# Rotary embedding on one core: first batch stored in three parts instead of five, and one signed GpSimd product per tile instead of two

## Chip, cores and metric

One core of one Trainium2 chip. The metric is the device time of one execution in microseconds (us); lower is better. The times are medians of several executions. Profiles come from one execution each; their span starts at the first instruction and is about 1.9 us shorter than the device time.

## The reference, cut to what matters

```python
x: (8, 2048, 8, 64) float32      # batch, sequence, heads, head width
cos, sin: (2048, 32) float32
x1, x2 = x[..., :32], x[..., 32:]
out1 = x1 * cos - x2 * sin
out2 = x1 * sin + x2 * cos
out  = concatenate([out1, out2], axis=-1)
```

The input is 33.55 MB, the output as much, and the two tables 0.52 MB. Each element needs two products and an add, so the work is thin beside the bytes.

## The kernel before

A batch is a tile of 128 partitions; a partition holds 16 sequence positions, a row of 32 KB (`ROW`). `HD` is one position (2 KB), `UNIT` four positions (8 KB a row). Batches live in five buffers (`NBUF`); a batch is rotated in place and stored from its buffer, so the load of batch b + 5 waits until batch b is stored. SyncE issues the loads, ScalarE the stores.

```python
cos_sb = const_pool.tile([P, R, Dh], f32, tag="cb")
sin_sb = const_pool.tile([P, R, Dh], f32, tag="sb")
nsin   = const_pool.tile([P, R, Dh], f32, tag="ns")
...
keep(nc.scalar.mul(nsin, sin_sb, -1.0))
...
def rotate(b, lo, n):            # one tile of 2 or 4 positions
    ...
    if kind != "C":              # GpSimd: t2 = swapped halves of x, times -sin and sin
        for u, tab in ((1, sin_sb), (0, nsin)):
            keep(nc.gpsimd.tensor_mul(
                out=t2u[:, :, u, :]..., in0=xu[:, :, 1 - u, :]..., in1=rep(tab[...], H)))
    keep(nc.vector.tensor_mul(out=t1..., in0=xk, in1=rep(cos_ps[...], 2 * H)))
    if kind == "A":
        keep(nc.vector.tensor_add(out=xt, in0=t1, in1=t2))
    ...                          # B: add on TensorE; C: both products on VectorE, add on TensorE

for b in range(B):
    done = 0
    outs = list(spans([2 * UNIT, UNIT, UNIT] if b == last else [ROW]))
    for lo, n in spans(pieces(b)):       # first batch: 2, 2, 4, 4, 4 positions
        rotate(b, lo, n)
        done = lo + n
        while outs and sum(outs[0]) <= done:
            whole = outs.pop(0)
            if b == 0:
                for part in spans([HD, HD, 2 * HD, UNIT, 2 * UNIT]):
                    store(b, *part)
            else:
                store(b, *whole)
    if b + NBUF <= last:
        load(b + NBUF)
```

Each tile's form is fixed per batch: most are "A"; five tiles are "B" or "C". `t1` of form A and the cosine table used by VectorE are in PSUM.

## Time and profile before

| | before |
|---|---|
| median | 163.64 us (3 runs, 163.50 to 163.69) |
| span of the profile | 161.9 us |
| VectorE busy | 140.1 us |
| GpSimd busy | 139.0 us |
| bytes moved | 67.65 MB, mean 418 GB/s |
| last add ends / last store lands | 152.5 / 161.0 us |

Three resources are busy nearly all the time. Which one sets the end is read from what is still at work last, and from what is queued when it starts: the prediction shows the strip of slices, the queues, the stretches and the waits for that. In these views PE is TensorE (PEld its weight loads), DVE VectorE, ACT ScalarE, POOL GpSimd and SP SyncE; a q behind the name is the engine's queue of instructions that only issue or wait. A line of a stretch has the stretch and its length, busy time and number of instructions of PE, PEld, DVE, ACT and POOL, the granted TensorE clock, the DMA share and GB/s.

### The profile page before, as it was taken

What the parts mean: (1) busy time and instruction counts of PE and PEld (TensorE: products, weight loads), DVE (VectorE), ACT (ScalarE), POOL (GpSimd) and SP (SyncE); (2) the same over time, 40 slices, a digit from 0 to 9 for tenths busy, and PEclk for the clock granted to TensorE, in tenths of its full rate; (3) what the DMA queues carried; (4) which work ended last, traced back from release to release, by engine and by line L of the source; (5) the groups of instructions that cost most, each with busy time, mean ns of one, the idle gap of its engine ahead of it and who ended that gap; (6) DMA issues with size and microseconds to landing.
All of it is one profiled execution on the core that took longest, in us unless ns stands there. A gap on an engine that the chain in (4) does not pass through costs nothing.

```text
span 161.9 us, 470 instructions
## 1 busy us (share of the span) xinstructions
PE 46.7 (29%) x80; PEld 18.6 (11%) x80; DVE 140.1 (87%) x66; ACT 14.4 (9%) x24; POOL 139.0 (86%) x70
## 2 busy tenths in 40 slices
PE   0000000498009950893039903970000000000000
PEld 0000000142004310340023402320000000000000
DVE  0468999999999999999999999999999999999600
ACT  3300000014000220041001210130000000000000
POOL 1299999999999899999994999999999999996000
PEclk9999999999955796599755985899555555555555
DMA  5999999999998989998999999989999999999994
GB/s 188 417 435 505 438 413 413 413 421 437 437 470 344 465 364 445 494 413 389 510 397 389 518 391 397 502 389 407 494 397 413 486 397 421 478 397 409 429 417 178
DMA packets 3746, 67.65 MB, mean 418 GB/s; under 512 B 416, under 2 KB 416, under 8 KB 1056
## 3 DMA queue, kind: packets, MB, share of 16 engines
q1 hardware_dynamic: 1728, 34.08, 49.6%
q10 hardware_dynamic: 2016, 33.56, 48.3%
q14 instruction: 2, 0.02, 0.0%
HBM read 34.08 MB, written 33.55 MB: 418 GB/s over the span
## 4 chain that ended last, share of the span: by engine, by line
DVE 75%; POOL 9%; issue 6%; DMA 3%; SPq 0%; DVEq 0%; POOLq 0%
DVE t L128 40%; DVE xt L135 33%; POOL t L121 9%; DMA sin_sb<-in_sin_dram 3%; DVE t L145 3%; DVEq L135 0%; SPq L69 0%; SPq L67 0%; POOLq L121 0%
## 5 line engine op out<-in xcount | busy, mean ns | idle before, releaser
L121 POOL TENSOR_TENSOR t<-xt,sin_sb 128x1024 f32<-128x1024 f32 (+1 forms) x32 | 71.1, 2222 | 8.6 <-DMA sin_sb<-in_sin_dram 5.6
L128 DVE TENSOR_TENSOR t<-xt,cos_ps 128x2048 f32<-128x2048 f32 (+1 forms) x34 | 73.4, 2167 | 0.8
L121 POOL TENSOR_TENSOR t<-xt,nsin 128x1024 f32<-128x1024 f32 (+1 forms) x32 | 71.2, 2225 | 0.0
L135 DVE TENSOR_TENSOR xt<-t,t 128x2048 f32<-128x2048 f32 (+1 forms) x29 | 62.2, 2145 | 5.4 <-POOL t L121 2.5
L140 PE MATMUL o<-t,eye 128*128 128x512 f32 x24 | 17.1, 804 | 25.0 <-DVE t L128 25.0
L156 PE MATMUL o<-t,eye 128*128 128x512 f32 x16 | 10.9, 786 | 36.6 <-DVE t L128 36.6
L141 PE MATMUL o<-t,eye 128*128 128x512 f32 x24 | 15.2, 719 | 0.0
L142 ACT COPY xt<-o 128x512 f32<-128x512 f32 x12 | 7.0, 586 | 46.5 <-PE o L141 46.5
L140 PEld LDWEIGHTS o<-t,eye 128*128 128x128 f32 x24 | 5.6, 250 | 33.4 <-issue 33.4
L161 ACT COPY xt<-o 128x512 f32<-128x512 f32 x8 | 4.7, 586 | 42.7 <-DVE t L128 26.6
L156 PEld LDWEIGHTS o<-t,eye 128*128 128x128 f32 x16 | 3.6, 248 | 41.5 <-POOL t L121 30.4
L141 PEld LDWEIGHTS o<-t,eye 128*128 128x128 f32 x24 | 6.0, 251 | 8.5 <-issue 8.5
L92 DVE COPY cos_ps<-cos_sb 128x512 f32<-128x512 f32 x1 | 0.7, 695 | 6.1 <-DMA cos_sb<-in_cos_dram 6.1
L157 PE MATMUL o<-t,neye 128*128 128x512 f32 x8 | 4.9, 722 | 0.2 <-DVE t L145 0.2
L145 DVE TENSOR_TENSOR t<-xt,sin_ps 128x2048 f32<-128x2048 f32 x2 | 4.6, 2280 | 0.0
L157 PE MATMUL o<-t,eye 128*128 128x512 f32 x8 | 4.1, 592 | 0.0
L157 PEld LDWEIGHTS o<-t,neye 128*128 128x128 f32 x8 | 1.8, 239 | 3.7 <-issue 3.7
L157 PEld LDWEIGHTS o<-t,eye 128*128 128x128 f32 x8 | 1.5, 190 | 1.9 <-issue 1.9
L89 ACT ACT_TABLE_LOAD x1 | 1.3, 1283 | 0.7 <-PEq L202 0.7
L89 ACT ACTIVATE nsin<-sin_sb 128x512 f32<-128x512 f32 x1 | 0.6, 630 | 4.8 <-DMA sin_sb<-in_sin_dram 4.8
L90 ACT COPY sin_ps<-sin_sb 128x512 f32<-128x512 f32 x1 | 0.6, 579 | 0.0
L79 POOL MEMSET eye<- 128x128 f32 x1 | 0.2, 205 | 0.3 <-POOLq L202 0.3
(6 smaller groups left out, 1.0 us busy)
## 6 DMA issues: line engine op xcount, KB each, us to landing
xt<-in_x_dram SPq DMA_DIRECT2D x7, 4096.0 KB, 26.7
out_dram<-xt ACTq DMA_DIRECT2D x6, 4096.0 KB, 33.3
out_dram<-xt ACTq DMA_DIRECT2D x2, 2048.0 KB, 24.3
out_dram<-xt ACTq DMA_DIRECT2D x3, 1024.0 KB, 11.2
xt<-in_x_dram SPq DMA_DIRECT2D x2, 1024.0 KB, 5.9
xt<-in_x_dram SPq DMA_DIRECT2D x1, 2048.0 KB, 11.4
out_dram<-xt ACTq DMA_DIRECT2D x2, 256.0 KB, 18.9
out_dram<-xt ACTq DMA_DIRECT2D x1, 512.0 KB, 32.6
```

What stands on the lines that cost most here:

```text
L89: keep(nc.scalar.mul(nsin, sin_sb, -1.0))
L92: keep(nc.vector.tensor_copy(cos_ps, cos_sb))
L121: nc.gpsimd.tensor_mul(out=t2u[:, :, u, :].rearrange("p (r h) d -> p r h d", h=H), in0=xu[:, :, 1 - u, :].rearrange("p (r h) d -> p r h d" ...
L128: nc.vector.tensor_mul(out=t1.rearrange("p (r k d) -> p r k d", r=nr, d=Dh), in0=xk, in1=rep(cos_ps[:, r0 : r0 + nr, :], 2 * H),)
L135: keep(nc.vector.tensor_add(out=xt, in0=t1, in1=t2))
L140: nc.tensor.matmul(o, eye, t1[:, cs], start=True, stop=False)
L141: nc.tensor.matmul(o, eye, t2[:, cs], start=False, stop=True)
L142: keep(nc.scalar.copy(xt[:, cs], o))
L145: nc.vector.tensor_mul(out=t2.rearrange("p (r k d) -> p r k d", r=nr, d=Dh), in0=xk, in1=rep(sin_ps[:, r0 : r0 + nr, :], 2 * H),)
L156: nc.tensor.matmul(o, eye, t1u[:, gs, u, :], start=True, stop=False)
L157: nc.tensor.matmul(o, eye if u else neye, t2u[:, gs, 1 - u, :], start=False, stop=True)
L161: nc.scalar.copy(xu[:, gs, u, :], o.rearrange("p (g d) -> p g d", d=Dh))
```

## The change

The intent: get the first batch out earlier and in fewer pieces, so that its buffer takes the sixth batch's load earlier; and halve GpSimd's instruction count by multiplying both swapped halves in one go with a table that holds -sin and sin side by side. Its space is found by letting the raw tables share rotating buffers.

```diff
-    cos_sb = const_pool.tile([P, R, Dh], f32, tag="cb")
-    sin_sb = const_pool.tile([P, R, Dh], f32, tag="sb")
-    nsin = const_pool.tile([P, R, Dh], f32, tag="ns")
+    cos_sb = t1s_pool.tile([P, R, Dh], f32, tag="t1s", name="cos_sb")
+    sin_sb = t1s_pool.tile([P, R, Dh], f32, tag="t1s", name="sin_sb")
+    sgn = const_pool.tile([P, R, 2, Dh], f32, tag="sg")
...
-    keep(nc.scalar.mul(nsin, sin_sb, -1.0))
+    for lo, hi in ((0, 4), (4, R)):
+        keep(nc.scalar.mul(sgn[:, lo:hi, 0, :], sin_sb[:, lo:hi, :], -1.0))
+        keep(nc.scalar.copy(sgn[:, lo:hi, 1, :], sin_sb[:, lo:hi, :]))
...
-            for u, tab in ((1, sin_sb), (0, nsin)):
-                keep(nc.gpsimd.tensor_mul(... one half ...))
+            keep(
+                nc.gpsimd.tensor_mul(
+                    out=t2.rearrange("p (r h u d) -> p r h u d", r=nr, h=H, u=2),
+                    in0=swapped(xt, nr),        # steps by -Dh between the halves
+                    in1=signed(sgn[:, r0 : r0 + nr, :, :], nr),
+                )
             )
...
+    def shares(b):
+        if b == 0:
+            return [HD, 7 * HD, 2 * UNIT]
...
-        outs = list(spans([2 * UNIT, UNIT, UNIT] if b == last else [ROW]))
+        outs = list(spans(shares(b)))
...
-                whole = outs.pop(0)
-                if b == 0:
-                    for part in spans([HD, HD, 2 * HD, UNIT, 2 * UNIT]):
-                        store(b, *part)
-                else:
-                    store(b, *whole)
+                store(b, *outs.pop(0))
```

More of the change, by code (lines that the diff above doesn't have):

```diff
@@ L95, in rep, with swapped, signed @@
         return dataclasses.replace(a, ap=[a.ap[0][:], a.ap[1][:], [0, n], a.ap[-1][:]])
+    def swapped(a, nr):
+        return dataclasses.replace(
+            a,
+            offset=a.offset + Dh,
+            ap=[a.ap[0][:], [HD, nr], [D, H], [-Dh, 2], [1, Dh]],
+        )
+    def signed(a, nr):
+        return dataclasses.replace(
+            a, ap=[a.ap[0][:], [D, nr], [0, H], [Dh, 2], [1, Dh]]
+        )
     kinds = {}
@@ L118, in rotate @@
         if kind != "C":
-            for u, tab in ((1, sin_sb), (0, nsin)):
-                keep(
-                    nc.gpsimd.tensor_mul(
-                        out=t2u[:, :, u, :].rearrange("p (r h) d -> p r h d", h=H),
-                        in0=xu[:, :, 1 - u, :].rearrange("p (r h) d -> p r h d", h=H),
-                        in1=rep(tab[:, r0 : r0 + nr, :], H),
-                    )
+            keep(
[3 more added lines that the diff above has]
+                    in1=signed(sgn[:, r0 : r0 + nr, :, :], nr),
                 )
+            )
         keep(
@@ L171, in pieces @@
         return [UNIT] * 4
+    def shares(b):
+        if b == 0:
+            return [HD, 7 * HD, 2 * UNIT]
+        if b == last:
+            return [2 * UNIT, UNIT, UNIT]
+        return [ROW]
     for b in range(B):
         done = 0
-        outs = list(spans([2 * UNIT, UNIT, UNIT] if b == last else [ROW]))
+        outs = list(spans(shares(b)))
         for lo, n in spans(pieces(b)):
```

## The prediction

> **What bounds the kernel now.** I read the strip of 40 slices first, then the DMA queues, then stretches of time, and only then the chain of waits, because the three busy rows compete for the title.
>
> ```profile
> DVE  0468999999999999999999999999999999999600
> POOL 1299999999999899999994999999999999996000
> DMA  5999999999998989998999999989999999999994
> DMA packets 3746, 67.65 MB, mean 418 GB/s; under 512 B 416, under 2 KB 416, under 8 KB 1056
> q1 hardware_dynamic: 1728, 34.08, 49.6%
> q10 hardware_dynamic: 2016, 33.56, 48.3%
> ```
>
> VectorE, GpSimd and the DMA engines all look full. But DVE and POOL end two to three slices (of 4.05 us) before the DMA row does, and the two DMA queues (q1 loads, q10 stores) together take 97.9% of 16 engines' span. Only 2.1% of 161.9 us, 3.4 us, is not covered by packets. The stretches say where that is (columns at the end: DMA share, GB/s):
>
> ```profile
> 2.00:14.00 12.00, 0.00 (x0) 0.00 (x0) 6.35 (x6) 1.37 (x4) 7.11 (x5) 1.00 1.03 429
> 44.00:58.00 14.00, 9.08 (x14) 3.85 (x15) 13.65 (x7) 1.76 (x3) 13.53 (x6) 0.63 0.96 398
> 66.00:124.00 58.00, 26.49 (x48) 10.61 (x46) 56.22 (x26) 7.04 (x12) 55.59 (x25) 0.74 1.01 434
> 124.00:152.00 28.00, 0.00 (x0) 0.00 (x0) 26.97 (x14) 0.00 (x0) 24.23 (x13) 0.50 1.00 430
> 159.00:162.00 3.00, 0.00 (x0) 0.00 (x0) 0.00 (x0) 0.00 (x0) 0.00 (x0) 0.50 0.19 79
> ```
>
> A packet is counted in the stretch in which it starts, so edges blur a little. The transfers run at about 430 GB/s from 2 us to 159 us, whether loads and stores mix (66 to 124) or only stores are left (124 to 152). 67.65 MB at the 434 of the long stretch are 155.9 us. The first packet starts at 1.7 us and the last ends at 160.6 us (packet records), 158.9 us: about 3 us above the ideal. By the packet records one part of those is 0.5 us of slow first rows at the head, another 0.55 us of stretched load rows, nearly all of it between 40 and 58 us (the 398 above), the rest row overhead and uneven ends of the 16 engines.
>
> The chain of waits says something else:
>
> ```profile
> DVE 75%; POOL 9%; issue 6%; DMA 3%; SPq 0%; DVEq 0%; POOLq 0%
> DVE t L128 40%; DVE xt L135 33%; POOL t L121 9%; DMA sin_sb<-in_sin_dram 3%; DVE t L145 3%; DVEq L135 0%; SPq L69 0%; SPq L67 0%; POOLq L121 0%
> ```
>
> It is a chain of compute and ends with the last add, at 152.5 us; that store's own time is the rest of the span. A 1 MB store needs 2.4 us at 434 GB/s, yet the last one lands 8.5 us after its issue (the shortest issue-to-landing time of any store), because earlier stores are queued before it. The DMA queue sets the end. Compute has about 3 to 5 us of slack: the last store has only to be in the queue when the one before it drains, at about 157 us.
>
> The first batch's stores, by issue and landing (KB each, us to landing), and SyncE's waits:
>
> ```profile
> 10.66 17.84 ACTq L74 DMA_DIRECT2D out_dram<-xt  x5
> out_dram<-xt ACTq DMA_DIRECT2D x1, 512.0 KB, 32.6
> out_dram<-xt ACTq DMA_DIRECT2D x1, 1024.0 KB, 39.8
> out_dram<-xt ACTq DMA_DIRECT2D x1, 2048.0 KB, 35.0
> SPq L67 <- DMA out_dram<-xt: 83.2, 4, 27.9
> ```
>
> The diff's loop looks as if it issued all five parts together after the batch, but the trace has them at 10.66, 11.06, 13.25, 18.71 and 28.16 us: each goes when its rows are done. They land at 24.7, 35.0, 45.9, 58.5 and 63.2 us, and the sixth batch's load, which needs that buffer, is issued only at 63.3.
>
> **What the Trainium skill says.** "DMA: Bandwidth & Descriptors", Queues, rings and completion order: each DMA engine takes turns between the queues it has work for, packet by packet. The trace agrees: beside 32 KB load rows, the second 256 KB of stores took 10.3 us (24.7 to 35.0), 25 GB/s, about the 2:32 share of 432. The same page, Where 436 GB/s comes from, gives a ceiling of 435 GB/s; the 434 measured here leaves nothing above it. "GPSIMD Engine Reference", Performance versus the Vector engine, has 4497 ns for an fp32 product of 2048; here 1024-element products start 2.28 us apart and 512-element ones 1.215, so a line through both gives 4.41 us for 2048. "SBUF — State Buffer", Who interferes with whom: a DVE instruction with two SBUF inputs contends with GpSimd. In the code each product and add of VectorE has one input in PSUM, and both take 2292 ns beside a busy GpSimd; the change leaves that so.
>
> **The change part by part.**
>
> *Store parts.* Five row sizes (2, 2, 4, 8, 16 KB) become three (2, 14, 16). No byte is saved. Rows: 128 per DMA, eight per engine, so 16 fewer rows on each engine. A 2 KB store row takes 84 ns and a 32 KB one 1213 ns in the packet records; the line through them has 8.7 ns per row: 16 x 8.7 = 0.14 us saved. Timing: the first part goes at about 11 us as before, lands near 25. The 14 KB part is ready with the third tile, near 18.7, and is at the head of the store queue from 25 on. A turn of an engine is then one load row (1.21 us) and one 14 KB row (0.54, from the line): 1.75, eight turns 14 us, landing near 40. The 16 KB part: 8 x 1.82 = 14.6, landing near 54.5. So the first batch's store is out some 8.5 us earlier, and the sixth load is issued near 55 instead of 63.3. The store-only gap (58 to 67 us) fills with loads, and the loads end later: I count 32 load rows per engine for batches 1 to 4, 25 of them sent by 54, the rest and the later loads in turns of 2.43 us with 32 KB stores. That puts the later loads near 91, 111 and 130 us, now 86.2, 106.3 and 125.8 us. VectorE wants them near 97, 114 and 133. Still in time, with thinner margins of 3 us. Work on the path saved: 0.14 us.
>
> *The slow stretch at 40 to 58 us.* 4 and 8 KB store rows alternate there with load rows, and some load rows take up to 1.74 us instead of 1.21. From 66 to 124, where rows of 32 KB alternate, this hardly occurs. If the small rows or the drained load queue cause it, the change takes away up to 0.55 us; I don't know the cause, so I count half, 0.25 us.
>
> *One product per tile.* Two products of 1024 (4.56 us start to start) become one of 2048 (4.41 by the line): 0.15 us per four-row tile. There are 28 pairs at 1024 and 4 pairs at 512: 28 x 0.15 + 4 x 0.15 = 4.8 us of GpSimd time. All beside the DMA queue: nothing at the end.
>
> *Signed table.* GpSimd's first product starts at 6.89, when the sine lands. It will wait for two ScalarE instructions of 128 elements a row (about 0.3 us each, as the 0.30 us negation of the 128x128 identity): start near 7.4. Its first product ends near 9.7 instead of 9.37; by the fourth tile the shorter products have made it up. First store some 0.3 us later, hidden: the first store packet starts at 14.6 us now although issued at 10.66, behind load rows already under way.
>
> *Tables in rotating buffers.* The cosine and sine tables use the buffers that the second batch's VectorE-only tile takes; their readers are done near 9 us, the tile starts at 28. No wait.
>
> Sum: 163.64 - 0.14 - 0.25 = 163.25; with rounding in the uneven tail, **163.2 us**.
>
> **Rivals.**
>
> 1. *GpSimd is slower with the swapped access.* The product now reads x with a step backwards between halves, one dimension more. For: nothing in this trace has that pattern. Against: runs of 32 contiguous elements stay. Slack absorbs about 4 us, 3% of GpSimd's 139; at 10% slower the end would go out by some 10 us, to 173.
>
> 2. *Loads come late.* The margins of 3 us on the last two loads are estimates. If they vanish, VectorE idles by a few us, and the slack at the end takes most of that: 163.5 to 165.
>
> 3. *Compute is the true bound, as the chain has it.* Then the saving on GpSimd and the earlier stores would shorten the end by 1 to 3 us, to 161 or 162. Against: from 124 us stores alone fill the engines, without a gap, until the last drains.
>
> 4. *Removing the small rows frees the whole loss in mid-kernel*: 162.9.
>
> **Range and chances.** The body moves only between -0.7 us (all of the stretch and the rows) and +0.5 (thin load margins); widened below by 0.3 for something of rival 3, 162.6 to 164.1 should hold it 8 times in 10. A gain of 2% needs 3.3 us, more than every idle moment of the DMA engines together: 0.02. A loss of 2% needs rival 1 or a new wait: 0.03. Within 2%: 0.95.
>
> **What would show it.** Right: DMA still near 430 GB/s throughout and 98% in the two queues; 1728 packets on the store queue (2016, less 256 rows, less 16 semaphore packets for each of the two DMAs saved); the first batch's last part landing near 54 us; the sixth load issued near 55; no store-only stretch at 58 to 67; GpSimd busy near 134 us; VectorE's last add still near 152. Wrong: a stretch after 20 us below 400 GB/s, GpSimd products well over 4.6 us, idle VectorE before the batches of 114 and 133 us, or a last store that lands less than 5 us after its issue, which would mean that compute had become the bound.

## More of the kernel before

One more line pair is needed later: the GpSimd groups before, kept apart by shape (times executed, then busy us and mean ns of one).

```profile
L121 POOL TENSOR_TENSOR t<-xt,nsin 128x1024 f32<-128x1024 f32 x28 | 66.1, 2360 | 0.0
L121 POOL TENSOR_TENSOR t<-xt,sin_sb 128x1024 f32<-128x1024 f32 x28 | 66.0, 2356 | 3.1 <-DVE xt L135 2.6
```

Consecutive products overlap a little, so busy time over count (66 / 28) slightly overstates what one costs.

## The result and the profile after

| | before | after |
|---|---|---|
| median, same rounds | 163.66 us (6 runs, 163.50 to 163.76) | 163.67 us (6 runs, 163.52 to 164.02) |
| ratio after / before | | 1.0004, 95% interval 0.9991 to 1.0018 |
| GpSimd busy | 139.0 us | 135.8 us |
| VectorE busy | 140.1 us | 140.1 us |
| first batch's last part lands | 63.2 us | 53.8 us |
| sixth load issued | 63.3 us | 53.8 us |
| last three loads land | 86.2, 106.3, 125.8 us | 92.4, 112.4, 131.7 us |
| last add ends / last store lands | 152.5 / 161.0 us | 153.3 / 160.8 us |

A ratio here is the mean time of one kernel's fast runs over that of the other's of the same rounds, so it isn't quite the ratio of the medians beside it.

The strip and the queues after:

```profile
DVE  0458999999999999999999899999999998999900
POOL 1199999999999799989995989997999969999100
DMA  5999999899999999999999998999999999999994
...
DMA packets 3457, 67.64 MB, mean 419 GB/s; under 512 B 384, under 2 KB 384, under 8 KB 768
...
q1 hardware_dynamic: 1728, 34.08, 49.7%
q10 hardware_dynamic: 1728, 33.56, 48.3%
```

The DMA row is as full as before (98.0% in the two queues, 97.9% before), with 1728 store packets where there were 2016. GpSimd's row has more gaps (the 5 to 8) than before: it is ahead and waits. In stretches, with GB/s in the last column:

```profile
22.00:26.00 4.00, 0.00 (x0) 0.00 (x0) 3.86 (x3) 0.00 (x0) 4.00 (x2) 1.00 0.94 336
44.00:58.00 14.00, 8.97 (x16) 3.75 (x16) 13.65 (x7) 1.76 (x3) 13.12 (x3) 0.67 1.00 431
66.00:124.00 58.00, 27.13 (x48) 10.77 (x46) 55.84 (x25) 7.04 (x12) 53.58 (x13) 0.74 1.01 434
124.00:152.00 28.00, 0.00 (x0) 0.00 (x0) 26.69 (x14) 0.00 (x0) 24.51 (x7) 0.50 1.00 430
```

The same four us in the kernel before:

```profile
22.00:26.00 4.00, 0.00 (x0) 0.00 (x0) 3.86 (x3) 0.00 (x0) 4.00 (x3) 1.00 0.98 418
```

The slow stretch that was at 44 to 58 us (398 GB/s) is gone from there (431), but a new one stands at 22 to 26 us (336 instead of 418). It moved. The last long stretches are as before.

The chain of waits names other things now:

```profile
DMA 46%; DVE 36%; POOL 8%; issue 4%; SPq 1%; ACT 0%; DVEq 0%; POOLq 0%; ACTq 0%
DMA xt<-in_x_dram 24%; DVE t L141 19%; DMA out_dram<-xt 18%; DVE xt L148 16%; POOL t L134 8%; DMA sin_sb<-in_sin_dram 3%; DVE t L158 1%; SPq L69 0%; SPq L67 0%; ACT sgn L91 0%; DVEq L148 0%; ACT sgn L90 0%; POOLq L134 0%; ACTq L74 0%
```

DVE 75% became DMA 46% with the same total: the chain follows whichever wait came last by a hair, and a load was now last where before a product was. I read it as a picture of a tie, not of a new bound; the experiments below test that. Where it hangs is in the waits and in the timeline near the last load:

```profile
POOL t L134 <- DMA xt<-in_x_dram: 3.7, 4, 1.4
DVE xt L148 <- POOL t L134: 3.4, 5, 1.6
```
```profile
131.85 4.51 POOL L134 TENSOR_TENSOR t<-xt,sgn 128x2048 f32<-128x2048 f32 x1 [1.41 <-DMA xt<-in_x_dram]
153.35 0.34 ACTq L74 DMA_DIRECT2D out_dram<-xt  x1
```

GpSimd waits 1.41 us for the last batch, which lands at 131.7, some 6 us later than before; the last store is issued at 153.35 instead of 152.5, and lands at 160.8 all the same. The GpSimd groups after:

```profile
L134 POOL TENSOR_TENSOR t<-xt,sgn 128x2048 f32<-128x2048 f32 x28 | 125.9, 4525 | 7.4 <-DVE xt L148 3.8 <-DMA xt<-in_x_dram 3.7
L134 POOL TENSOR_TENSOR t<-xt,sgn 128x1024 f32<-128x1024 f32 x4 | 9.3, 2346 | 6.0 <-ACT sgn L91 6.0
```

The 28 big tiles take 125.9 us instead of 66.1 + 66.0, some 6 us less by busy time; but the two-instruction form overlapped itself, and the total of GpSimd fell by 3.2 us (139.0 to 135.8).

### The profile page after: what moved, and what is told of

Read it like the earlier page. It is cut to its first block, busy times and chain, and to the rows that moved or that the text cites. A ratio compares the mean times of both kernels' runs of the same rounds, so it can differ in the third digit from the quotient of the medians.

```text
span 161.6 us, 440 instructions
## 1 busy us (share of the span) xinstructions
PE 47.1 (29%) x80; PEld 18.7 (12%) x80; DVE 140.1 (87%) x66; ACT 15.1 (9%) x27; POOL 135.8 (84%) x38
## 3 DMA queue, kind: packets, MB, share of 16 engines
q1 hardware_dynamic: 1728, 34.08, 49.7%
q10 hardware_dynamic: 1728, 33.56, 48.3%
## 4 chain that ended last, share of the span: by engine, by line
DMA 46%; DVE 36%; POOL 8%; issue 4%; SPq 1%; ACT 0%; DVEq 0%; POOLq 0%; ACTq 0%
DMA xt<-in_x_dram 24%; DVE t L141 19%; DMA out_dram<-xt 18%; DVE xt L148 16%; POOL t L134 8%; DMA sin_sb<-in_sin_dram 3%; DVE t L158 1%; SPq L69 0%; SPq L67 0%; ACT sgn L91 0%; DVEq L148 0%; ACT sgn L90 0%; POOLq L134 0%; ACTq L74 0%
## 5 line engine op out<-in xcount | busy, mean ns | idle before, releaser
L134 POOL TENSOR_TENSOR t<-xt,sgn 128x2048 f32<-128x2048 f32 (+1 forms) x32 | 135.1, 4253 | 13.5 <-ACT sgn L91 6.0
L170 PE MATMUL o<-t,neye 128*128 128x512 f32 x8 | 5.7, 830 | 0.2 <-DVE t L158 0.2
L90 ACT ACTIVATE sgn<-sin_sb 128x128 f32<-128x128 f32 (+1 forms) x2 | 0.8, 413 | 4.8 <-DMA sin_sb<-in_sin_dram 4.8
L91 ACT COPY sgn<-sin_sb 128x128 f32<-128x128 f32 (+1 forms) x2 | 0.8, 388 | 0.0
```

The source lines that it names most:

```text
L90: keep(nc.scalar.mul(sgn[:, lo:hi, 0, :], sin_sb[:, lo:hi, :], -1.0))
L91: keep(nc.scalar.copy(sgn[:, lo:hi, 1, :], sin_sb[:, lo:hi, :]))
L134: nc.gpsimd.tensor_mul(out=t2.rearrange("p (r h u d) -> p r h u d", r=nr, h=H, u=2), in0=swapped(xt, nr), in1=signed(sgn[:, r0 : r0 + nr, ...
L170: nc.tensor.matmul(o, eye if u else neye, t2u[:, gs, 1 - u, :], start=False, stop=True)
```

## Experiments

Twelve runs on two chips, in three calls; each call has its own runs of the kernel before (11 each). Theory: the transfers set the end, so the bytes and the cost of the rows are all that counts, and compute has some us of slack. Rivals: the compute chain sets it; or the two halves of the change have opposite effects that cancel.

| run | median us | ratio to before, 95% interval |
|---|---|---|
| stores_only | 163.42 | 0.9973 (0.9938 to 1.0007) |
| product_only | 165.42 | 1.0078 (1.0033 to 1.0123) |
| product_again | 165.51 | 1.0085 (1.0037 to 1.0132) |
| after_again | 163.86 | 0.9996 (0.9969 to 1.0024) |
| copy_only | 163.04 | 0.9942 (0.9902 to 0.9983) |
| less_1mb | 161.16 | 0.9829 (0.9782 to 0.9876) |
| dve_plus1 | 163.57 | 0.9988 (0.9957 to 1.0019) |
| dve_plus4 | 169.83 | 1.0393 (1.0338 to 1.0447) |
| few_stores_before | 158.89 | 0.9693 (0.9647 to 0.9740) |
| few_stores_after | 159.37 | 0.9722 (0.9667 to 0.9776) |
| one_part | 164.64 | 1.0043 (1.0004 to 1.0082) |
| rows_2k | 183.86 | 1.1190 (1.1118 to 1.1262) |

The intervals are wider than in the first comparison because the kernel before scattered more on these chips (medians 163.83, 163.58 and 163.66; single runs up to 166.0). The medians are of all runs, the ratios of those marked fast. Four runs were marked slow, which here means only over 1.5% above the fastest of the same kernel, with a clock (0.731 to 0.745) like that of the others: one each of product_again, after_again, rows_2k and the kernel before.

### What sets the end: copy_only, less_1mb

The changed kernel without the rotation, and with 1 MB less to store:

```diff
         for lo, n in spans(pieces(b)):
-            rotate(b, lo, n)
             done = lo + n
```
```diff
+        if b == 3:
+            return [3 * UNIT]
         return [ROW]
```

> The changed kernel without any rotation: every batch is loaded and stored as it came (wrong result on purpose), same DMAs with the same rows. My theory: the transfers alone need nearly all of the time, 161 to 163.5 us. Rival B: the time falls well below, to 157 us or less, since VectorE's 146 us chain with its head and tail is gone.

> The changed kernel, but the fourth batch stores only three of its four tiles: 1 MB less to write (wrong result on purpose), all the compute kept. My theory: 1.05 MB at 433 GB/s, so 2.4 us less (161.2). Rival B: no change, since no instruction of the chain is gone.

Without any rotation: 163.04 us (162.97 to 163.14). Its page:

```profile
DVE  0100000000000000000000000000000000000000
DMA  5999999999999999999999999999999999999895
```

VectorE is idle, and the kernel is only 0.6 us faster than with 140 us of work on it. So all compute together costs some 0.6 us of the end (163.67 is of another call; the kernel before of this call is 0.8 us above). Taking away 1.05 MB took 2.5 us (163.67 to 161.16; 2.4 expected), with all compute kept, so it was not the compute chain. Their outputs are wrong, which doesn't matter for the times.

### How much slack compute has: dve_plus1, dve_plus4

One extra product on VectorE, for the first or for all four tiles of the seventh batch:

```diff
+        if b == 6 and lo == 0:           # dve_plus4: if b == 6
+            keep(nc.vector.tensor_mul(out=t1..., in0=xk, in1=rep(cos_ps[...], 2 * H)))
         if kind == "A":
```

> The changed kernel with one extra VectorE product of 2.29 us on the first tile of the seventh batch, late in the kernel (result unchanged). Transfers set the end: the last store is issued near 155.6 instead of 153.35, the store before it drains near 158, so the time stays within 0.3 us of the changed kernel. Rival (the compute chain sets the end): 2.3 us longer.

> The same extra product on all four tiles of the seventh batch, 9.2 us of VectorE (result unchanged). If transfers set the end with a slack of about 3 us in compute: the last add ends near 162.5, its store lands some 4.5 us later, so 168 to 169.5, about 5 us more. Rival (the compute chain sets the end): 9 us more, 172.5 or above.

With 2.29 us more on VectorE, late and on the chain: 163.57 us, against 163.86 of the unchanged kernel. Nothing. The last issue and its time to landing (KB, us):

```profile
155.37 0.34 ACTq L74 DMA_DIRECT2D out_dram<-xt  x1
out_dram<-xt ACTq DMA_DIRECT2D x1, 1024.0 KB, 5.3
```

The store is issued 2.0 us later and lands at 160.7, as before: it spent less time in the queue, 5.3 us instead of 7.4. That is the plainest sign of a wait that is not on the path. With 9.2 us more, 169.83 us: some 6 us came through (168 to 169.5 were expected, so the slack was a little less than I had reckoned, or the runs of 170.6 and 171.0 had another cause; only the run of 168.9 has a profile). In that one the last add ends at 162.3 and its store lands 3.9 us later. Compute sets the end there.

### What the product change is worth if compute does set the end: few_stores_before, few_stores_after

```diff
     def store(b, lo, n):
+        if 1 <= b <= 5:
+            return
```

> The kernel before without the stores of batches 1 to 5 (wrong result on purpose): 21 MB less to write, so the transfers need only some 110 us and compute must set the end. VectorE's last add near 152.3 as now, its store lands some 4 us later: 158 to 159.5 us in all. A time near 163 would mean that something else than transfers held the kernel.

> The changed kernel with the same stores left out (wrong result on purpose). VectorE's 140 us of work are the same, and GpSimd was not ahead of it by need: within 0.7 us of few_stores_before although GpSimd has 3 us less to do. If GpSimd is what paces compute (rival): 2 to 3 us faster than few_stores_before.

158.89 and 159.37 us: 0.5 us slower with the change, within the 0.7 expected. Page of the changed kernel with these stores left out:

```profile
DVE  0459899999999999999999989999999999999970
DMA  5999999998999999999999920000000000997945
```

Now the DMA row is empty for some ten slices and VectorE's row is what is full to the end. GpSimd's 3 us are worth nothing even here, since VectorE has its 140 us to do whatever GpSimd does. What remains is probably the later start: in the profiles of the whole kernels the first add starts at 9.73 us with the change and at 9.40 before, because the signed table has to be built first; here the last add ends 0.4 us later (152.55 against 152.15).

So the two floors lie close: 163.0 for the transfers, 158.9 for compute. Neither half of the change lowers the higher one.

### Do the two halves cancel: stores_only, product_only, and again

stores_only is the kernel before with the diff's `shares(b)` part alone; product_only has the tables and the merged product, and the old store loop:

```diff
-        outs = list(spans(shares(b)))
+        outs = list(spans([2 * UNIT, UNIT, UNIT] if b == last else [ROW]))
...
+                    for part in spans([HD, HD, 2 * HD, UNIT, 2 * UNIT]):
+                        store(b, *part)
```

> The store split alone (2, 14, 16 KB), with the two GpSimd products of before. Transfers set the end (my theory): within 0.3% of before, the 0.14 us of saved rows at most; the first batch's last part lands near 54 us instead of 63.2. Rival A (two opposite effects that cancel in the full change): the split alone would be faster by 0.5 us or more, and the product alone slower by as much. Rival B (the compute chain sets the end): the same time too, since GpSimd and VectorE work is unchanged.

> One GpSimd product per tile and the signed table alone, with the five store parts of before. My theory: within 0.3% of before, although GpSimd is busy about 3 us less. Rival A: slower by 0.5 us or more. Rival B (compute chain sets the end): faster by 1 us or more, as GpSimd's products are then on the chain.

The product alone was slower by 0.8%, which is against my theory and for rival A; the split alone was 0.3% faster, with an interval that includes no difference. The profile of product_only shows where: not in compute, whose last add ends at 153.0 (153.3 in the changed kernel). The end of the transfers, in 1 us stretches (GB/s last):

```profile
159.00:160.00 1.00, 0.00 (x0) 0.00 (x0) 0.00 (x0) 0.00 (x0) 0.00 (x0) 0.50 0.66 279
160.00:161.00 1.00, 0.00 (x0) 0.00 (x0) 0.00 (x0) 0.00 (x0) 0.00 (x0) 0.50 0.18 74
161.00:162.00 1.00, 0.00 (x0) 0.00 (x0) 0.00 (x0) 0.00 (x0) 0.00 (x0) 0.50 0.06 25
162.00:163.00 1.00, 0.00 (x0) 0.00 (x0) 0.00 (x0) 0.00 (x0) 0.00 (x0) 0.50 0.04 16
```

For the last 2 us a single DMA engine or two are at work (0.06 = one sixteenth); the changed kernel has 0.02 at 160 to 161 and nothing after. The last store lands at 163.0, when the last of its engines is done. The packet records name no engine, but they can be chained, each to the one that ended where it starts. So chained, two engines had two 32 KB store rows each of 1.97 to 2.42 us instead of 1.21, starting between 65.8 and 68.1 us (not one engine with four, as the text for product_again below has it); the last packets end 3.0 us after the bulk. This is just where, in the five-part kernels, only stores are in flight (58 to 67 us) and the sixth load sets in. I ran it again beside the changed kernel, unaltered:

> The same kernel as product_only, once more. In its first profile one DMA engine had four 32 KB store rows of about 2.4 us instead of 1.21 between 65 and 71 us, just after a stretch in which only stores were in flight, and finished 2 to 3 us after the others. If that belongs to the five-part stores with the merged product (theory S): again 0.5 to 1% slower than before, most runs above 164.5. If it is chance of that chip or moment (theory C): within 0.3% of before, with a few runs of either kernel above 164.5.

> The changed kernel once more, beside the same runs of before. Under theory S (the single late engine needs the store-only stretch, which only the five-part kernels have) all runs stay within 163.3 to 164.1 while before now and then exceeds 164.2. Under theory C it has as many late runs as before.

It repeated on the other chip (165.51), and again engines were late, four this time, at the same place, though that profile fell in a run marked slow (166.2). Over all fast runs with the whole compute, those above 164.2 us are: product_only and product_again 9 of 11; the kernel before 8 of 38; the three-part kernels (after, after_again, stores_only, dve_plus1) 0 of 21. With the runs marked slow, which may well be late for the same reason, they are 10 of 12, 9 of 39 and 1 of 22. That one is a run of after_again at 165.99, so the three-part form isn't proof against it; it missed the 164.1 I had set for theory S.

What follows: the two halves do interact. With five parts the merged product often ends late; with three parts it did once in 16 runs. In both profiles (product_only and product_again) the slow rows were on exactly the engines that had begun their first 32 KB store row before 62.3 us; in the profile of before the earliest began at 62.4 and none was slow. Why a row then takes twice as long, and why the merged product brings it on more often, is open. That the store-only stretch is needed isn't shown; the one late three-part run speaks against it, and has no profile.

### What the split itself does: one_part, rows_2k

```diff
         if b == 0:
-            return [HD, 7 * HD, 2 * UNIT]
+            return [ROW]
```
```diff
-        return [ROW]                     # batches 1 to 6
+        return [HD] * 16
```

> The changed kernel with the first batch stored in one part of 32 KB rows when all of it is computed, near 28 us. The engines have loads to move until then, so by my theory the same time within 0.3% of before: how the first batch's store is cut is worth nothing but its rows. If storing early pays: 0.5 us or more slower than the changed kernel.

> The changed kernel with batches 1 to 6 stored in sixteen parts of 2 KB rows each: the same bytes, 15 x 8 x 6 = 720 more rows on each DMA engine. At 8.7 ns per row, if the engines stay busy: 6.3 us more, near 170. If a row's cost is nothing, or hidden beside loads: within 0.5 us of the changed kernel. More than 173: the many stores wait for each other's semaphores and the queue runs dry.

One part: 164.64 us, with six runs within 0.2 us, and that is 1.0 us over the changed kernel's 163.67, and over the median of the kernel before (the ratio is 1.0043 because late runs raise the mean of the kernel before). My "worth nothing but its rows" was wrong; it matters how the first batch is cut. In stretches:

```profile
14.00:28.00 14.00, 0.00 (x0) 0.00 (x0) 13.09 (x6) 0.00 (x0) 14.00 (x4) 1.00 1.00 428
28.00:34.00 6.00, 3.02 (x3) 1.00 (x4) 6.00 (x4) 0.00 (x0) 6.00 (x2) 1.00 0.95 317
34.00:66.00 32.00, 15.77 (x31) 6.67 (x30) 31.24 (x15) 4.68 (x8) 30.37 (x8) 0.84 1.02 440
```

The slow stretch sits at 28 to 34 us, right before this kernel's first store rows (33.1 us and later). That suggests a pattern in the packet records: load rows are stretched in the 2 to 4 us before the first rows of a larger store part. In the table, the time lost is what load rows took above their usual time (1213 ns for 32 KB), per engine:

| kernel | store rows grow | stretched load rows at | lost, us per engine |
|---|---|---|---|
| before | 4 to 8 KB, at 46.3 us | 43 to 46 us | 0.13 |
| before | 8 to 16 KB, at 57.6 | 54 to 57 | 0.31 |
| after | 2 to 14 KB, at 25.5 | 22 to 25 | 0.61 |
| copy_only | 2 to 14 KB, at 18.0 | 16 to 19 | 0.35 |
| one_part | none to 32 KB, at 33.1 | 29 to 34 | 1.3 |

Every profile of a five-part kernel has the stretch where before has it, and every one of a three-part kernel where after has it; copy_only, whose stores come earlier, has it earlier. So neither compute nor chance makes it. The pattern isn't clean: copy_only loses another 0.23 us at 25 to 27 us, with no larger part ahead. rows_2k, below, speaks against it more: after 60 us its load rows lose another 3.7 us per engine though no store row ahead is above 2 KB, about 2.4 us in the last load rows before stretches of stores alone and 1.2 us in the first ones after them. In the kernel before, too, the loss at 54 to 57 us falls on the last load rows before only stores are left, so there the drained load queue is a rival to the larger part. For 22 to 25 us in the changed kernel, where loads go on, it is not. An estimate fits its size roughly: if an engine takes in one store row ahead, the extra bytes at its 27 GB/s (a 32 KB row in 1.21 us) are 0.15 us for 4 KB, 0.3 for 8, 0.45 for 12 and 1.2 for 32. But the step from 16 to 32 KB, at 54 us in the changed kernel, shows no loss, and rows_2k doesn't fit, so this is a guess and the cause is open.

rows_2k: 183.86 us, the third branch of what I expected. A 2 KB row still takes 84 ns as a rule, so at the usual times the rows of an engine grew by the 6.3 us (157.0 to 163.3). But the time that an engine's packets really took grew by 11.9 us (158.4 to 170.4): stretched rows, of loads mostly, are another 4.9 us, and semaphore packets 0.8. The last packet ends 20.9 us later (181.3 instead of 160.4), so the other 9 us are queues running dry (the low digits of the DMA row):

```profile
DMA  6998989999999989999999999999990799992955
q10 hardware_dynamic: 14688, 33.56, 47.3%
q1 hardware_dynamic: 1728, 34.08, 46.0%
```
```profile
ACT xt L155 <- DMA out_dram<-xt: 49.4, 3, 20.6
```

ScalarE issues the stores and also copies TensorE's sums back. With 96 stores in its stream for these six batches, where there were six, its copies waited for stores, up to 20.6 us at a time, and what needs these copies waited behind them. What each store itself waited for (a semaphore shared with an earlier DMA, as I had expected) wasn't looked at. So of the 20 us about a third is the usual cost of the rows; the rest came with the many stores in other ways.

## Why the prediction was right, and where it wasn't

163.2 us within 162.6 to 164.1 was predicted, 163.67 measured; right, for the reason given. One piece of it was luck: the product was to cost nothing, and product_only shows that it costs 0.8% beside five store parts. Only together with the three parts, as here, does it cost nothing, and the prediction didn't foresee that. By its steps:

- **The bound** (transfers; compute with 3 to 5 us of slack). Right: copy_only is 0.6 us faster, 1 MB less is 2.5 us faster, 2.3 us more on VectorE is nothing, 9.2 us more is 6. The chain of waits, which pointed at compute with 75%, misled as supposed.
- **Timing of the parts.** Near: landing at 24.9, 39.3 and 53.8 us where 25, 40 and 54.5 were reckoned; the sixth load at 53.8 (55); late loads landing at 92.4, 112.4 and 131.7 (91, 111, 130). Alternating turns of one load row and one store row describe it to 1.7 us. The margins were thinner than the 3 us named: GpSimd waited 1.41 us for the last load, and the last add came 0.8 us later. The slack took it.
- **Rows saved, 0.14 us.** The rows are gone (1728 packets, as foretold), which is the 0.14 us at their usual times. The measured sum of an engine's packet times fell by 0.10 us, as the stretched rows differ a little too. It is too little to see in the time, whose interval is from -0.15 to +0.3 us.
- **The slow stretch, 0.25 us.** This is the term that failed. It was put down as half likely to vanish with the small rows; it moved to 22 to 26 us and lost about as much (0.63 instead of 0.55 us per engine). Of its two causes, the small rows and the drained load queue, neither is needed: one_part has no small store rows before its stretch and goes on loading after it, and it loses the most (1.3 us). The loss moves with the cut of the first batch's stores; its cause is open. A stretch below 400 GB/s after 20 us was one of the prediction's own signs of being wrong, and it came. Without this term the sum is 163.5.
- **GpSimd, 4.8 us saved.** Oversized: 3.2 measured. The line through the two start-to-start times gave 4.41 us for a 2048 product; where nothing waits they start 4.47 us apart (busy time over count is 125.9 / 28 = 4.50). The Trainium skill, "GPSIMD Engine Reference", Performance versus the Vector engine, has 4497 ns for an fp32 add of 2048 elements; the product here takes as long. Off the path, so without effect, and few_stores shows that it would be even if compute set the end.
- **Signed table.** First product at 7.35 (7.4 foretold), first add 0.33 us later; hidden.
- **Rivals.** GpSimd with the swapped access is not slower beyond the 0.06 us by which the line missed. Late loads came in part and were absorbed. Compute as the bound is refuted. What no rival named are the late single engines, to which both profiles of the product beside five parts trace its 0.8%. The late runs of the kernel before have no profile; that they have the same source isn't shown.

## What to carry to other kernels

When several engines look full, ask which of them still has work queued when the others end, then take one thing away at a time: a run with the compute removed gives the floor of the transfers, and tells at once what rearranging compute could be worth (here 0.6 us). Getting the first batch stored some 9 us earlier moved load and store traffic about but brought nothing here, as the DMA queues together were hardly ever empty; storing nothing of it until all was done (one_part) cost 1.0 us. Look at the scatter as well as the median: here a single late engine held the last store back by some 2 us, and the schedule in which the load queue doesn't stand empty in mid-kernel had fewer late runs (1 of 22, against 9 of 39).

## What the Trainium skill lacked or had wrong

- "DMA: Bandwidth & Descriptors", Queues, rings and completion order: it says that an engine drains about 9 to 17 descriptors of one queue before it switches. In the changed kernel it switched after every row of the two queues: eight 2 KB store rows beside 32 KB load rows took from 14.5 to 24.3 us, turns of about 1.3 us (1.21 + 0.084) and the 0.6 us of stretched rows, and whole-batch rows alternated one for one. How many descriptors a row is the profile doesn't record, so the 9 to 17 can't be called wrong; what the page lacks is that a turn here is one row, of 2 KB or of 32.
- The same page, Where 436 GB/s comes from, has about 358 GB/s of HBM bind for transfers between HBM and SBUF. (Its own table has 425 for a core alone.) One core alone held 428 to 434 GB/s here from 26 to 159 us, with loads and stores mixed or stores alone, well above the 358.
- No page: load rows of 32 KB were stretched in places, 0.13 to 1.3 us per engine each, often just before a larger store part on the other queue (4 to 8 KB up to none to 32 KB), in rows_2k around stretches of stores alone.
- No page: single DMA engines ran rows at half rate for some 4 us (2.4 instead of 1.21 us for 32 KB) in the two profiles of the product beside five parts, whose last stores land 2 us later. (The DMA page does say that two of the engines are usually slower; the packet records name no engine, but in one profile four were late.)
- No page has the cost of one more row at this size (the DMA page has a cost per packet for far smaller ones): 8.7 ns per engine by the packet records, 6.3 us for 720 more rows at their usual time. In rows_2k the engines' packet time grew by 11.9 us in all.
